# The low halves of the first expert table's 128 chunks, subtracted on GpSimd in place of VectorE

## The chip, the cores and the metric

The kernel runs on one core of a Trainium2 chip. The metric is device time in microseconds (us). The engines are called by the profile's names: PE (TensorE matmuls), PEld (TensorE weight loads), DVE (VectorE), ACT (ScalarE), POOL (GpSimd) and SP (the engine that issues most DMAs).

## The reference, cut to what matters

One layer of a latent-token backbone: two token mixers (retention and RG-LRU) over 512 latent and 256 context tokens, then a PEER feed-forward net with 16384 one-neuron experts, of which each token uses 16 in each of 8 heads. The change lies in that last part:

```
s1, i1 = lax.top_k(s[:, :, 0], K);  s2, i2 = lax.top_k(s[:, :, 1], K)
cand = (s1[..., :, None] + s2[..., None, :]).reshape(PEER_BLOCK, PEER_HEADS, K * K)
top, ci = lax.top_k(cand, K)
e = i1[ci // K] * PEER_NKEYS + i2[ci % K]          # shortened
g = jax.nn.softmax(top, axis=-1)
act = jax.nn.gelu(jnp.einsum('thkd,td->thk', u_tab[e], xb))
return jnp.einsum('thk,thkd->td', g * act, v_tab[e])
```

`u_tab` is the first table and `v_tab` the second; each has 16384 rows of 1024 floats.

## The kernel before, in words

Matmuls run in a 32-bit format of reduced precision (fp32r). To keep precision every operand x is split in two: `split` (L60) has ACT copy x rounded into a high half (L61) and DVE subtract that from x for the low half (L62). `mm3` (L64) then makes three products, high by high (L65), high by low (L66) and low by high (L67).

After the mixers (until about 640 us) the expert part has three stages.

- **Key scores and top 16** (about 680 to 820 us). PE makes the queries and the scores; DVE finds the 16 best of each half and of the pairs (`top16`, L644, and `top_pairs`, L657).
- **One-hot blocks** (822 to 1050 us). For three of the four tiles of 128 tokens the routing weights are spread into a dense table `wd`. Each tile is one block of eight groups of 16 tokens: DVE builds four one-hot tensors for a group (L887 to L890, 128x2048 fp16), PE multiplies them in 32 small products (L896, L897, into `pw`), and ACT copies these out (L898). Between the second and third block stands the preparation of the fourth token tile (`gather_prep`, L779).
- **Output** (1055 to 1850 us). For 128 chunks of 128 experts each, PE adds act times v into three output tiles (`po`, 18 products of 512 columns for a chunk). DVE makes `af` (L969) and the low halves `al` and `vwl` of it (L62). The fourth token tile is worked on beside that: POOL gathers single rows of the tables by indirect DMA into four `row` buffers (L801, L809) and DVE uses them (L803, L814).

The first table is not gathered for the three tiles but worked through densely: `s_stage` (L750) loads chunk j (512 KB, tile `w`, two buffers), splits it into `wh` and `wl` (four buffers each), makes 24 products of 384 columns into `pS` (two PSUM buffers) and has ACT apply the gelu (`gt`, L756). These 128 chunks, called S chunks here, are spread over all three stages. In the first two they fill PE between other work; in the output stage there is one for about two output chunks.

Code order doesn't set the order on the engines: a scheduler orders every engine's instructions when the kernel is built, by its own model of their cost, and each engine then works through its list in order. Buffers come free when the last reader is done. So SP's next load of a `w` tile waits for both readers of the old one, ACT's copy and the subtraction; SP works in order too.

Of the kernel before, what the change touches and what calls it, by code (L numbers as in the profile page):

```python
# [17 lines left out]
OP = mybir.AluOpType  # L18
# [34 lines left out]
def block_kernel(ctx: ExitStack, tc: tile.TileContext, A):  # L53
    nc = tc.nc
    V, S, PE, G, SY = nc.vector, nc.scalar, nc.tensor, nc.gpsimd, nc.sync

    def f(ap):
        return ap.bitcast(F32)

    def split(hi, lo, src):  # L60
        S.activation(hi, src, AF.Copy)  # L61
        V.tensor_tensor(lo, src, f(hi), op=OP.subtract)  # L62

    def mm3(out, wh, wl, xh, xl, start, stop):  # L64
        PE.matmul(out, wh, xh, start=start, stop=False)  # L65
        PE.matmul(out, wh, xl, start=False, stop=False)  # L66
        PE.matmul(out, wl, xh, start=False, stop=stop)  # L67
# [5 lines left out]
    wst = ctx.enter_context(tc.tile_pool(name="wst", bufs=2, reuse_waits="tile"))  # L73
    wsp = ctx.enter_context(tc.tile_pool(name="wsp", bufs=4, reuse_waits="tile"))
# [5 lines left out]
            return psA.tile([128, 1024], F32, name=name, tag="ps2")  # L80
        return psA.tile([128, 512], F32, name=name, tag="ps1", bufs=2)

    def load_split(src, st, sp):
        n, m = src.shape[1:]
        w = st.tile([128, n, m], F32, name="w", tag="w")
        SY.dma_start(w, src)
        wh = sp.tile([128, n, m], F32R, name="wh", tag="wh")
        wl = sp.tile([128, n, m], F32R, name="wl", tag="wl")
        split(wh, wl, w)
        return wh, wl  # L90


# [13 lines left out]
    def prefetch(n):  # L106
        while plan and len(ahead) < n:
            ahead.append(load_split(plan.pop(0), wst, wsp))
# [43 lines left out]
    st = sstk.enter_context(tc.tile_pool(name="start", bufs=1, reuse_waits="tile"))  # L152
# [95 lines left out]
    sp = const.tile([128, 24], F32, name="sp")  # L248
# [52 lines left out]
    def lru_in(c, pu, pp):  # L301
        u = lp.tile([128, NT], F32, name="u")
        S.activation(u, pu[:, :NT], AF.Identity, scale=col("conv_w", 16 + c), bias=col("conv_b", c))
        for tap, sh in ((0, 2), (1, 1), (3, -1)):
            for lo, hi in ((0, NX), (NX, NT)):
                if sh > 0:
                    o, i = u[:, lo + sh:hi], pu[:, lo:hi - sh]
                else:
                    o, i = u[:, lo:hi + sh], pu[:, lo - sh:hi]
                V.scalar_tensor_tensor(o, i, col("conv_w", 8 * tap + c), o, op0=OP.mult, op1=OP.add)  # L310
        uh = lp.tile([128, NT], F32R, name="uh")
        ul = lp.tile([128, NT], F32R, name="ul")
        split(uh, ul, u)
        x5 = lp.tile([128, NX], F32, name="x5", tag="q")
        S.activation(x5, pp, AF.Copy)
        g5 = lp.tile([128, NX], F32, name="g5")
        S.activation(g5, x5, AF.Square)
        V.tensor_scalar(g5, g5, 0.044715, 1.0, op0=OP.mult, op1=OP.add)
        V.tensor_tensor(g5, g5, x5, op=OP.mult)
        S.activation(g5, g5, AF.Tanh, scale=math.sqrt(2.0 / math.pi))  # L320
        V.scalar_tensor_tensor(g5, g5, 1.0, x5, op0=OP.add, op1=OP.mult)
        return u, uh, ul, g5
# [38 lines left out]
    def rope_split(hi, lo, p, scale=1.0):  # L361
        x = rp.tile([128, NX], F32, name="rx", tag="P", bufs=2)
        t = rp.tile([128, NX], F32, name="rt", bufs=1)
        S.activation(x, p[:, :NX], AF.Copy, scale=scale)
        for a in (0, 64):
            b = 64 - a
            V.tensor_tensor(t[a:a + 64], x[b:b + 64], ssin[b:b + 64], op=OP.mult)
        V.tensor_tensor(x, x, cos, op=OP.mult)
        V.tensor_tensor(x, x, t, op=OP.add)
        split(hi, lo, x)  # L370
# [165 lines left out]
    with ExitStack() as es:  # L536
# [53 lines left out]
        for q, (pool, th, tl) in enumerate(((lm, "lruh", "lrul"), (mg, "reth", "retl"))):  # L590
            wo.append([pool.tile([128, 4, KT, 128], F32R, name=f"wo{t}", tag=t, bufs=1) for t in (th, tl)])
            for c in range(4):
                w = wst.tile([128, KT, 128], F32, name="w", tag="w")
# [6 lines left out]
        for hf in range(2):  # L600
            if hf:
                wqs = [load_split(A["wq"][i], wst, wsp) for i in range(HG)]
            tk = slice(HN * hf, HN * hf + HN)
            ps = ps_of("ps_ss2", psW)
            for c in range(KT):
                pm = ps_of("pout", psS)
                wh, wl = (t[:, c % 4] for t in wo[c // 4])
# [141 lines left out]

    def s_stage(j):  # L750
        ps = psS.tile([128, 512], F32, name="pS")
        uh, ul = load_split(A["uT"][j], wst, wsp)
        for k in range(KT):
            mm3(ps[:, :DT], uh[:, k], ul[:, k], h2h[:, k, :DT], h2l[:, k, :DT], k == 0, k == KT - 1)
        gt = pb.tile([128, DT], F32, name="gt", bufs=RING)
        S.activation(gt, ps[:, :DT], AF.Gelu_apprx_tanh)  # L756
        if j < SPILL:
            SY.dma_start(gd[:, j], gt)
        else:
            Gs[j] = gt  # L760
# [3 lines left out]
    def s_more(n=1):  # L764
        nonlocal s_next
        for _ in range(n):
            if s_next < 128:
                s_stage(s_next)
                s_next += 1
# [284 lines left out]
```

## Time and profile before

| | us |
|---|---|
| median of 3 runs | 1881.03 (1879.26 to 1882.01) |
| profiled execution | 1879.51 |
| its span | 1877.7 |

The profile has the share of each engine in the span, the stretches in which it is busy, for every group of instructions its number, its mean time and what ended the idle time before it, and the waits of one engine on another. A matmul's time in a row is its length in a pipeline and overlaps the next one's; what one costs is the distance between starts. A mean granted TensorE clock of 1.00 is full speed.

### The profile page before, as it was taken

How to read it: one execution, taken by the hardware profiler on the slowest of the kernel's cores; microseconds unless marked ns; L12 is line 12 of the kernel's file. 1: busy time of each engine (PE TensorE's matmuls, PEld its weight loads, DVE VectorE, ACT ScalarE, POOL GpSimd, SP SyncE). 2: the span in 40 equal slices, each digit the busy share in tenths (PEclk: the TensorE clock that was granted, in tenths of full speed). 3: DMA queues.
4: the chain of work that ended last, by engine and by line, in shares of the span. 5: the costliest groups of instructions: out<-in, count | busy, mean ns of one | idle time of the engine just before them, and what ended most of it. 6: DMA issues, size and time to landing. Idle time of an engine off the chain costs nothing.

```text
span 1877.7 us, 26999 instructions
## 1 busy us (share of the span) xinstructions
PE 1820.2 (97%) x9969; PEld 1603.0 (85%) x9969; DVE 1512.3 (81%) x2801; ACT 824.3 (44%) x1213; POOL 375.7 (20%) x327
## 2 busy tenths in 40 slices
PE   7899999999999999999999999999999999999997
PEld 3788888887888989999999988888887888888885
DVE  8987878788844579999988578886786879788688
ACT  4667575765222444445545333333333333333333
POOL 0000000000000000000022134443443535445350
PEclk9999999999999999999999999999999999999999
DMA  7122121225943433567778999998989999999986
GB/s 310 52 67 68 57 68 57 68 64 189 335 136 115 138 108 115 184 193 238 261 283 299 317 345 328 345 336 298 323 324 312 346 340 337 347 331 355 319 302 208
DMA packets 175753, 432.72 MB, mean 230 GB/s; under 512 B 14082, under 2 KB 87170, under 8 KB 171140
## 3 DMA queue, kind: packets, MB, share of 16 engines
q1 hardware_dynamic: 138756, 296.75, 46.7%
q0 software_dynamic: 36864, 134.23, 19.7%
q8 instruction: 78, 1.28, 0.3%
q14 instruction: 55, 0.45, 0.1%
HBM read 389.32 MB, written 41.62 MB: 229 GB/s over the span
## 4 chain that ended last, share of the span: by engine, by line
PE 74%; DVE 11%; DMA 9%; ACT 3%; issue 2%; SPq 1%; DVEq 0%; ACTq 0%
PE po L65 8%; PE po L66 8%; PE po L67 8%; PE pS L65 7%; PE pS L66 7%; PE pS L67 7%; DMA wt<-wd 4%; DMA vw<-in_v_dram 2%; DVE wl L62 2%; PE pgm L65 1%; PE pgm L66 1%; PE pgm L67 1%; PE pmm L66 1%; PE pmm L67 1%; PE pmm L65 1%
## 5 line engine op out<-in xcount | busy, mean ns | idle before, releaser
L61 ACT ACTIVATE wh<-w 128x1024 fp32r<-128x1024 f32 (+1 forms) x216 | 224.8, 1043 | 369.0 <-DMA w<-in_uT_dram 105.0
L65 PE MATMUL pS<-h2h,wh 128*128 128x384 f32 x1024 | 347.1, 339 | 7.0 <-ACT gt L756 6.7
L67 PE MATMUL pS<-h2h,wl 128*128 128x384 f32 x1024 | 346.1, 338 | 0.7 <-DVE wl L62 0.7
L66 PE MATMUL pS<-h2l,wh 128*128 128x384 f32 x1024 | 346.2, 338 | 0.0
L62 DVE TENSOR_TENSOR wl<-w,wh 128x1024 fp32r<-128x1024 f32 (+1 forms) x216 | 259.0, 1200 | 88.2 <-ACT wh L61 87.5
L801 POOL DMA_INDIRECT row<-in_u_dram,ei x128 | 181.9, 1421 | 609.7 <-DVE row L803 316.0
L66 PE MATMUL po<-vwl,ah 128*128 128x512 f32 x768 | 299.9, 391 | 1.2 <-DVE vwl L62 1.2
L67 PE MATMUL po<-vwh,al 128*128 128x512 f32 x768 | 298.9, 390 | 0.0
L65 PE MATMUL po<-vwh,ah 128*128 128x512 f32 x768 | 271.5, 395 | 10.0 <-ACT vwh L61 8.1
L61 ACT ACTIVATE ah<-af 128x384 fp32r<-128x384 f32 x128 | 67.2, 525 | 387.0 <-PE po L66 220.2
L809 POOL DMA_INDIRECT row<-in_v_dram,ei x128 | 183.9, 1436 | 208.5 <-DVE acc L814 175.2
L65 PEld LDWEIGHTS pS<-h2h,wh 128*128 128x128 f32 x1024 | 193.2, 189 | 14.3 <-ACT gt L756 8.4
L67 PEld LDWEIGHTS pS<-h2h,wl 128*128 128x128 f32 x1024 | 193.1, 189 | 6.0 <-DVE wl L62 1.0
L66 PEld LDWEIGHTS pS<-h2l,wh 128*128 128x128 f32 x1024 | 193.3, 189 | 4.3
L62 DVE TENSOR_TENSOR vwl<-vw,vwh 128x1024 fp32r<-128x1024 f32 x128 | 156.1, 1220 | 27.1 <-ACT vwh L61 25.6
L65 PEld LDWEIGHTS po<-vwh,ah 128*128 128x128 f32 x768 | 143.1, 188 | 38.4 <-ACT vwh L61 10.6
L814 DVE SCALAR_TENSOR_TENSOR acc<-row,act,acc 128x1024 f32<-128x1024 f32 x127 | 162.7, 1281 | 14.0 <-DMA row<-in_v_dram,ei 13.4
L66 PEld LDWEIGHTS po<-vwl,ah 128*128 128x128 f32 x768 | 144.4, 188 | 29.9 <-DVE vwl L62 2.3
L67 PEld LDWEIGHTS po<-vwh,al 128*128 128x128 f32 x768 | 144.4, 188 | 27.8 <-DVE al L62 0.2
L61 ACT ACTIVATE vwh<-vw 128x1024 fp32r<-128x1024 f32 x128 | 134.4, 1051 | 61.6 <-DMA vw<-in_v_dram 59.9
L803 DVE SCALAR_TENSOR_TENSOR row<-row,h2t 128x1024 f32<-128x1024 f32 x128 | 153.8, 1220 | 2.4 <-DMA row<-in_u_dram,ei 2.4
L62 DVE TENSOR_TENSOR al<-af,ah 128x384 fp32r<-128x384 f32 x128 | 71.0, 554 | 62.6 <-ACT ah L61 57.5
(372 smaller groups left out, 3505.8 us busy)
## 6 DMA issues: line engine op xcount, KB each, us to landing
w<-in_uT_dram SPq DMA_DIRECT2D x128, 512.0 KB
vw<-in_v_dram SPq DMA_DIRECT2D x128, 512.0 KB
w<-in_w_in_dram SPq DMA_DIRECT2D x48, 512.0 KB
wd<-stg SPq DMA_DIRECT2D x24, 1024.0 KB
modb<-in_mod_t_dram SPq DMA_DIRECT2D x32, 512.0 KB
wt<-wd SPq DMA_DIRECT2D x9, 1536.0 KB
gd<-gt SPq DMA_DIRECT2D x57, 192.0 KB
gr<-gd SPq DMA_DIRECT2D x57, 192.0 KB
```

The source lines that it names most:

```text
L61: S.activation(hi, src, AF.Copy)
L62: V.tensor_tensor(lo, src, f(hi), op=OP.subtract)
L65: PE.matmul(out, wh, xh, start=start, stop=False)
L66: PE.matmul(out, wh, xl, start=False, stop=False)
L67: PE.matmul(out, wl, xh, start=False, stop=stop)
L801: G.indirect_dma_start(out=row, out_offset=None, in_=A["u"], in_offset=bass.IndirectOffsetOnAxis(ap=ei[:, j:j + 1], axis=0))
L803: V.scalar_tensor_tensor(row, row, 1.0, h2t, op0=OP.mult, op1=OP.mult, accum_out=act[:, j:j + 1])
L809: G.indirect_dma_start(out=row, out_offset=None, in_=A["v"], in_offset=bass.IndirectOffsetOnAxis(ap=ei[:, j:j + 1], axis=0))
L814: V.scalar_tensor_tensor(acc, row, act[:, j:j + 1], acc, op0=OP.mult, op1=OP.add)
```

## The change

`split` and `load_split` take an engine, and `s_stage` gives POOL for it. All other splits stay with DVE.

```
-    def split(hi, lo, src):
+    def split(hi, lo, src, eng=None):
         S.activation(hi, src, AF.Copy)
-        V.tensor_tensor(lo, src, f(hi), op=OP.subtract)
+        (eng or V).tensor_tensor(lo, src, f(hi), op=OP.subtract)
...
-    def load_split(src, st, sp):
+    def load_split(src, st, sp, eng=None):
...
-        split(wh, wl, w)
+        split(wh, wl, w, eng)
         return wh, wl
...
-        uh, ul = load_split(A["uT"][j], wst, wsp)
+        uh, ul = load_split(A["uT"][j], wst, wsp, G)
```

The scheduler lays out the instructions anew on all engines from the first S chunk on. On POOL the list after the start-up was nothing but gathers:

```order
L849 IOTA iof 128x128
L801 DMA row<-in_u_dram,ei 128x1024 x128
L809 DMA row<-in_v_dram,ei 128x1024 x128
L1050 UNCONDITIONAL_BRANCH
L1050 ISA
```

Now, in the first two stages, with `wl` the low half of an S chunk, it reads:

```order
L849 IOTA iof 128x128
L62 TENSOR_TENSOR wl<-w,wh 128x1024 x33
L801 DMA row<-in_u_dram,ei 128x1024 x4
L62 TENSOR_TENSOR wl<-w,wh 128x1024 x15
L801 DMA row<-in_u_dram,ei 128x1024 x2
L62 TENSOR_TENSOR wl<-w,wh 128x1024 x2
L801 DMA row<-in_u_dram,ei 128x1024
L62 TENSOR_TENSOR wl<-w,wh 128x1024
```

The first 33 subtractions stand ahead of the first gather, and from then on gathers and subtractions share the list; in the output stage one subtraction stands behind each three to five gathers.

On DVE, at the third group of the first one-hot block, the list was this (`ohB`, `ohAl` and `ohAh` are the one-hot tensors; `top`, `ci`, `cscr`, `prod`, `e` and `b` belong to the pair search of the next tile):

```order
L887 TENSOR_TENSOR ohB<-iota,e2T 128x2048
L888 TENSOR_TENSOR ohAl<-iota,e1T 128x2048
L647 MATCH_REPLACE cscr<-top,cand 128x50
L709 TENSOR_TENSOR prod<-mask,nlens 128x512
L890 TENSOR_TENSOR ohAl<-ohAl,glT 128x2048
L691 TENSOR_TENSOR prod<-prod 128x256
L647 MATCH_REPLACE cscr<-top,cand 128x50
L62 TENSOR_TENSOR wl<-w,wh 128x1024
L889 TENSOR_TENSOR ohAh<-ohAl,ghT 128x2048
L648 MAX top<-cscr 128x8
L691 TENSOR_TENSOR prod<-prod 128x256
L691 TENSOR_TENSOR prod<-prod 128x128
```

At that group it now reads:

```order
L887 TENSOR_TENSOR ohB<-iota,e2T 128x2048
L888 TENSOR_TENSOR ohAl<-iota,e1T 128x2048
L647 MATCH_REPLACE cscr<-top,cand 128x50
L648 MAX top<-cscr 128x8
L691 TENSOR_TENSOR prod<-prod 128x128
L693 TENSOR_TENSOR e_8001<-prod 128x64
L889 TENSOR_TENSOR ohAh<-ohAl,ghT 128x2048
L648 MAX top<-cscr 128x8
L649 MAX_INDEX ci<-top,cscr 128x8
L693 TENSOR_TENSOR b<-prod 128x64
L890 TENSOR_TENSOR ohAl<-ohAl,glT 128x2048
L649 MAX_INDEX ci<-top,cscr 128x8
```

The low half `wl` between the builds is gone, and DVE's list is otherwise of the same kinds of row. PE's list has the same products, in another order. The table says how many S chunks stand in it ahead of a place:

| S chunks ahead of | before | now |
|---|---|---|
| the first product of one-hot block 1 | 23.6 | 17.4 |
| the first product of block 2 | 39.2 | 29.4 |
| the first product of block 3 | 52.4 | 46.0 |
| the first product of the output stage | 67.9 | 66.4 |

In the output stage both lists mix the two kinds of chunk alike. There the gather that a subtraction stands right behind can start when a `row` buffer is free, which takes a DVE instruction that stands some four output chunks ahead of PE's use of that `wl`.

## Rows read from the trace of the kernel before

**Rows 1.** The page, part 1: busy us (share of the span) and count.

```profile
PE 1820.2 (97%) x9969; PEld 1603.0 (85%) x9969; DVE 1512.3 (81%) x2801; ACT 824.3 (44%) x1213; POOL 375.7 (20%) x327
```

**Rows 2.** Stretches: length, busy us (count) of each engine, clock, DMA, GB/s.

```profile
822.00:902.00 80.00, 80.00 (x624) 76.47 (x623) 79.22 (x226) 45.35 (x74) 0.00 (x0) 1.00 0.73 246
902.00:974.00 72.00, 72.00 (x591) 69.34 (x590) 65.02 (x98) 35.27 (x61) 10.51 (x4) 1.00 0.78 280
974.00:1050.00 76.00, 76.00 (x604) 73.95 (x604) 63.28 (x67) 37.28 (x62) 16.86 (x10) 1.00 0.81 284
...
1100.00:1800.00 700.00, 690.76 (x3320) 605.56 (x3319) 562.16 (x716) 244.29 (x334) 305.43 (x219) 1.00 0.94 331
```

**Rows 3.** The same stretches, DVE on tile wl alone: length, busy us (count).

```profile
822.00:902.00 80.00, 18.19 (x15) 1.00 0.73 246
902.00:974.00 72.00, 15.88 (x13) 1.00 0.78 280
974.00:1050.00 76.00, 17.75 (x15) 1.00 0.81 284
...
1100.00:1800.00 700.00, 65.90 (x54) 1.00 0.94 331
```

**Rows 4.** PE's waits, 640 us to the end: total us, times, longest.

```profile
PE po L65 <- ACT vwh L61: 8.1, 6, 2.7
PE pS L65 <- ACT gt L756: 6.7, 4, 4.1
...
PE pS L67 <- DVE wl L62: 0.7, 1, 0.7
...
PE pps L839 <- ACT sc L841: 0.2, 1, 0.2
```

**Rows 5.** PE in order of time, three places: start, length, instruction.

```profile
840.49 0.33 PE L66 MATMUL pS<-h2l,wh 128*128 128x384 f32 x1
...
841.53 0.33 PE L66 MATMUL pS<-h2l,wh 128*128 128x384 f32 x1
...
848.10 0.23 PE L897 MATMUL pw<-ohAl,ohB 128*128 128x128 f16 x1
...
848.40 0.22 PE L896 MATMUL pw<-ohAh,ohB 128*128 128x128 f16 x1
```

**Rows 6.** DVE groups: shapes, count | busy us, mean ns | idle before, releaser.

```profile
L62 DVE TENSOR_TENSOR wl<-w,wh 128x1024 fp32r<-128x1024 f32 x208 | 253.5, 1220 | 77.8 <-ACT wh L61 77.2 <-PE pw L897 0.3
...
L890 DVE TENSOR_TENSOR ohAl<-ohAl,glT 128x2048 f16<-128x2048 f16 x8 | 9.7, 1220 | 0.0
...
L812 DVE TENSOR_SCALAR acc<-row,act 128x1024 f32<-128x1024 f32 x1 | 0.8, 755 | 0.0
```

**Rows 7.** POOL groups, whole span.

```profile
L801 POOL DMA_INDIRECT row<-in_u_dram,ei x128 | 181.9, 1421 | 609.7 <-DVE row L803 316.0 <-PE pw L897 280.7 <-issue 11.8
L378 POOL IOTA dist<- 128x320 f32 x8 | 3.2, 400 | 17.8 <-DVE dt L388 9.2 <-ACT sc L396 5.7 <-ACT dt L395 2.9
L378 POOL IOTA dist<- 128x512 f32 x4 | 2.2, 560 | 11.7 <-ACT sx L383 11.7
```

**Rows 8.** S chunks finished, 736 to 800 us; what ACT's wh waited for.

```profile
L756 ACT ACTIVATE gt<-pS x13: 470/473/491, 739.8 to 798.5; 128x384 f32<-128x384 f32 x13
...
  DMA w<-in_uT_dram: 25.7, 10
```

**Rows 9.** POOL in order of time, two gathers: start, length [idle before <-releaser].

```profile
976.77 1.68 POOL L801 DMA_INDIRECT row<-in_u_dram,ei  x1 [30.70 <-DVE row L803]
...
1065.34 1.02 POOL L801 DMA_INDIRECT row<-in_u_dram,ei  x1 [25.66 <-DVE row L803]
```

**Rows 10.** DVE groups, 1100 to 1800 us: idle before, and its releasers.

```profile
L62 DVE TENSOR_TENSOR vwl<-vw,vwh 128x1024 fp32r<-128x1024 f32 x111 | 135.4, 1220 | 25.0 <-ACT vwh L61 23.5 <-issue 1.3
...
L969 DVE TENSOR_TENSOR af<-gt,wt 128x384 f32<-128x384 f32 x61 | 33.9, 555 | 27.1 <-DMA wt<-wd 26.0
```

## The prediction

> **What bounds the kernel now.** I read the shares first, then the stretches, then PE's waits. PE is busy for 97% of the span [rows 1], and in the three one-hot blocks and the output stage for all or nearly all of it: 80.00 of 80, 72.00 of 72, 76.00 of 76, 690.76 of 700 us [rows 2]. DVE is nearly as full in the first one-hot block (79.22 of 80 us) but not later (562.16 of 700 us). From 640 us on, PE's waits are eleven rows, from 8.1 us down to 0.2, some 23 us in all [rows 4]. The largest two end on ACT, behind transfers and table loads; the low half of an S chunk has one row, 0.7 us. So PE's own work sets the time, DVE is its close second in one place, and a lighter DVE can return little: that is the first thing to see.
>
> Is PE at its pace while it is busy? Six S products take 841.53 - 840.49 = 1.04 us, 0.173 us each, so a chunk of 24 needs 4.16 us. Five one-hot products take 0.30 us, 0.06 each, so a group's 32 need 1.9 us and a block's eight groups 15.2 us [rows 5]. Block 1 held 15.6 chunks before: 15.6 x 4.16 + 15.2 = 80.1 us, against 80 measured. PE runs there at its pace. In the top-16 stage it does not: twelve chunk intervals took 798.5 - 739.8 = 58.7 us, 4.89 each [rows 8], 0.73 us over the pace and 8.8 us in all.
>
> **The change, part by part.** Removed: 128 subtractions of 1.22 us on DVE [rows 6], 156 us of DVE work. As PE waits for them by 0.7 us in all [rows 4], almost nothing of that lies on the path.
>
> Added: 128 subtractions on POOL. The trace has no POOL instruction that reads a tensor. The nearest rows are the two index fills, 400 ns for 320 elements and 560 for 512 [rows 7]: 0.83 ns for an element written, and about 0.13 us fixed. One stream of 1024 is then 1.0 us, the lower end; two reads and a write one after the other are 2.7 us, the upper end. Two reads one after the other, with the write beside them, would be 1.8. I take 2.3, between the last two, since it moves three streams where the fills move one. (The Trainium skill, "GPSIMD Engine Reference", section 3.1, has 4497 ns for 2048 elements of such an instruction; half of it is an estimate of 2.25 us, with which the sum would be the same. No run here shows it yet.) On POOL's own time this fits: in the output stage it is busy for 305.43 of 700 us, and 54 subtractions add 124 us. An S chunk takes PE 4.16 us at the fastest, so 2.3 us keeps up.
>
> The unknown is whether DVE is held up while POOL reads. In the trace they never read side by side. DVE with two tensor operands takes 1220 ns for 1024 elements, with one 755 ns [rows 6]: the second operand's read is what limits it, so a further reader of the same partitions is likelier to take turns with it than to be free. The lower bound is no hold at all, the upper one is the whole POOL instruction for each chunk. I take turns on DVE's two-operand work only. In block 1 the 32 builds of four kinds, 9.7 us each [rows 6], are 38.8 of DVE's 61 us without `wl`, 64%, and much of the small work has two operands as well; I take 80%.
>
> Block 1 now: DVE's other work is 79.22 - 18.19 = 61.0 us [rows 2, 3]. PE has 12.0 chunks there in place of 15.6: 12.0 x 4.16 + 15.2 = 65.1 us. Without holds DVE still fits. With them it needs 61.0 + 12.0 x 2.3 x 0.8 = 83.1 us, **18.0 us more than PE**, and PE waits for one-hot tensors. PE's order is fixed, so it can't take later chunks in the meantime. The ends are 0, and at 2.7 us and 100% 61.0 + 32.4 - 65.1 = 28.3.
>
> Block 2: DVE 65.02 - 15.88 = 49.1 us; PE 16.6 chunks, 84.3 us. With holds 49.1 + 30.5 = 79.6 us, covered; at the upper end 93.9, so 0 to 9.6. Block 3 (to the first output product): DVE 63.28 - 17.75 = 45.5; PE 20.4 chunks, 100 us; with holds 83, covered, at the upper end 100.6, so 0 to 0.6. DVE's slack is that cover; if the holds were longer still, each further us would reach PE.
>
> Output stage: DVE 562.16 - 65.90 = 496.3 us, and 54 x 2.3 = 124 make 620 of 700. Some of its idle time ends on transfers, the 25.0 and 27.1 us of [rows 10], and can't be used; that gives 672, so it fits, with little room. Chance meetings of the two engines will pass through the two buffers of each operand now and then: I take 5 us, from 0 to 10.
>
> Top-16 stage: DVE's instructions there mostly have one tensor operand, so holds are taken as nothing. What it gives: a `w` buffer is now freed by POOL, which has nothing else to do, and not after DVE's queue, and ACT had waited 25.7 us for these loads [rows 8]. I take 4 of the 8.8 us lost to the pace, from 0 to 9. The other waits that end on DVE could give some 3 us more at best.
>
> Sum: 18.0 + 0 + 0 + 5 - 4 = +19 us on the profiled run's 1879.51 us, which is its span of 1877.7 and 1.8 around it. The median of the runs is 1.5 us longer, 1881.03, so **1900 us**. The ends: no hold and all gains, -12, 1869; the upper price and full holds, 28.3 + 9.6 + 0.6 + 10 = +48.5, 1929.
>
> A rule of the skill bears on this. In "SBUF — State Buffer", section "Who interferes with whom", a DVE instruction with two SBUF inputs and a POOL instruction that reads SBUF share a read path, and the second to start waits until the first is done. By that rule the holds are whole, and the sum is the one above rather than the lower end. No trace of before shows it: the gathers, POOL's only work beside a busy DVE, leave DVE's 1220 ns as they are.
>
> **The rivals.** *POOL's list holds the chunks up* (slower still). POOL waits at a gather until DVE has freed a `row` buffer, 30.70 and 25.66 us at two places [rows 9], and subtractions stand behind such gathers now, with SP's next `w` load behind these. Four `wl` buffers are a lead of four chunks, about 4 x 5 = 20 us with one-hot products between. Beyond that PE stops: 10.7 + 5.7 = 16 us on top, 1916 us. For it: waits over 20 us decide, and they are there. Against it: the scheduler placed gathers by the time at which it expects them to start, and in the output stage the lead is four output chunks.
>
> *No hold* (faster). DVE and POOL read without meeting. Then block 1 fits (61.0 against 65.1), the output stage has 134 us more DVE room, and the top-16 gain stays, with 4 us of other waits: -8, 1873 us. For it: nothing in the trace shows a meeting. Against it: the 755 against 1220 ns. It decides for faster as soon as a POOL subtraction costs DVE less than (65.1 - 61.0) / 12 = 0.34 us.
>
> *No difference.* The subtractions leave DVE as the change says, but the path is PE's work, which is the same to the last product; a short hold, about 0.6 us for each chunk of block 1 (3 us of waiting), cancels the gain: 1881 us.
>
> **How the numbers follow.** Holds as taken: 0.50, 1900 us. POOL's list: 0.15, 1916. No hold: 0.22, 1873. No difference: 0.13, 1881. A difference under 0.2%, 3.8 us, is about what a measurement of this kernel can't tell from none. That gives slower 0.65, same 0.13, faster 0.22. The range reaches from 1868, the lower end with all gains, to 1929, the upper price with full holds; a POOL list that jams and longer holds together lie outside, as does a DVE relief larger than PE's waits.
>
> **What would show it.** In the trace after: POOL's `wl` group near 2.3 us, longer beside one-hot builds; DVE's one-hot rows longer than 1220 ns, or gaps between them that end on nothing else; PE rows `pw` waiting for `ohB`, `ohAh` or `ohAl`, some 18 us, mostly in block 1; chunk intervals in the top-16 stage near 4.2 to 4.5 us. One-hot rows still at 1220 ns without gaps would mean no hold. PE waiting on `wl` from POOL by over 10 us, behind gathers that wait for L803, would be the second case. The forecast is wrong if the output stage takes more than some 10 us extra, since its cover was counted as holding.

## The result, and the profile after

The changed kernel takes **1968.2 us** (median of 4 runs, 1961.9 to 1972.9) beside 1881.5 us before (4 runs, 1879.3 to 1883.0): a ratio of 1.046, with a 95% interval of 1.044 to 1.049. Slower was forecast, but by 19 us; it is 87, and outside the range. The profiled execution has a span of 1960.1 us, 82.4 us more than before.

The page's first part, busy us and share of the span, answers [rows 1]:

```profile
PE 1838.0 (94%) x9969; PEld 1614.3 (82%) x9969; DVE 1567.6 (80%) x2673; ACT 824.2 (42%) x1213; POOL 704.9 (36%) x455
```

DVE lost 128 instructions, 156 us of work, and is busy for 55 us *longer* than before. So what is left on it must have grown by some 210 us. The groups of POOL and DVE (shapes and count | busy us, mean ns | idle before, with its releasers), which answer [rows 6, 7], show where:

```profile
L62 POOL TENSOR_TENSOR wl<-w,wh 128x1024 fp32r<-128x1024 f32 x128 | 329.2, 2574 | 287.5 <-ACT wh L61 285.0 <-PE pps L839 1.7
...
L803 DVE SCALAR_TENSOR_TENSOR row<-row,h2t 128x1024 f32<-128x1024 f32 x128 | 187.6, 1492 | 19.0 <-DMA row<-in_u_dram,ei 19.0
L814 DVE SCALAR_TENSOR_TENSOR acc<-row,act,acc 128x1024 f32<-128x1024 f32 x127 | 187.3, 1475 | 20.4 <-DMA row<-in_v_dram,ei 19.6
L62 DVE TENSOR_TENSOR al<-af,ah 128x384 fp32r<-128x384 f32 x128 | 91.5, 715 | 29.8 <-ACT ah L61 29.8
L889 DVE TENSOR_TENSOR ohAh<-ohAl,ghT 128x2048 f16<-128x2048 f16 x24 | 46.9, 1963 | 0.1
L890 DVE TENSOR_TENSOR ohAl<-ohAl,glT 128x2048 f16<-128x2048 f16 x24 | 39.5, 1657 | 0.2
L646 DVE FIND_INDEX8 idx<-vals,sc 128x8 uint32<-128x128 f32 x64 | 17.7, 284 | 0.0
L648 DVE MAX8 vals<-tscr 128x8 f32<-128x128 f32 x64 | 15.9, 277 | 0.0
```

The same view of the kernel before, two of these groups:

```profile
L803 DVE SCALAR_TENSOR_TENSOR row<-row,h2t 128x1024 f32<-128x1024 f32 x128 | 153.8, 1220 | 2.4 <-DMA row<-in_u_dram,ei 2.4
...
L646 DVE FIND_INDEX8 idx<-vals,sc 128x8 uint32<-128x128 f32 x64 | 17.4, 280 | 0.0
```

A build of a one-hot tensor had 1220 ns [rows 6] and has 1657 to 1963. The dot products of the gathered rows (L803) had 1220 as well and have 1492. The searches with one tensor operand (L646, L648) keep their 277 to 284 ns. Among these groups only work with two tensor operands has grown, and it has grown in busy time, not in the idle time before it: the instruction is counted as running while it is held.

Two stretches in order of time (start, length, instruction, idle before it) show how. First DVE, then POOL, in the first one-hot block:

```profile
849.96 1.21 DVE L888 TENSOR_TENSOR ohAl<-iota,e1T 128x2048 f16<-128x2048 f16 x1
851.09 0.68 DVE L717 TENSOR_TENSOR prod<-mask,dif 128x1024 f16<-128x1024 f16 x1
851.70 0.46 DVE L684 CAST cf<-ci 128x128 f16<-128x128 uint32 x1
851.83 0.76 DVE L645 MAX8 top<-cand 128x8 f32<-128x50 f32 x6
...
852.93 2.42 DVE L889 TENSOR_TENSOR ohAh<-ohAl,ghT 128x2048 f16<-128x2048 f16 x1
...
855.60 2.36 DVE L681 COPY dif<-lst 128x16 f16<-128x16 f16 x1
```

```profile
850.44 3.82 POOL L62 TENSOR_TENSOR wl<-w,wh 128x1024 fp32r<-128x1024 f32 x1 [4.44 <-ACT wh L61]
855.27 2.65 POOL L62 TENSOR_TENSOR wl<-w,wh 128x1024 fp32r<-128x1024 f32 x1 [1.02 <-ACT wh L61]
```

The first POOL subtraction ends at 850.44 + 3.82 = 854.26. Undisturbed ones have 2.36 us, so it did its work from 851.90 on: it had waited for DVE's L888 and L717, the later of which ends at 851.77. DVE's one-operand MAX8 ran beside it. L889 came at 852.93, was held until about 854.26, and then did its own work of 1.1 to 1.2 us: it ends at 855.35. The second subtraction ends at 857.92, and a DVE copy of 16 elements for each partition, 0.16 us at its fastest, stands for 2.36 us beside it. Each engine waits until the other's instruction is done, whole.

PE's waits from 640 us on (us in total, times, longest), against [rows 4]:

```profile
PE po L65 <- ACT vwh L61: 27.3, 14, 5.3
PE pS L65 <- ACT gt L756: 14.8, 7, 5.1
PE pw L897 <- DVE ohAl L890: 13.0, 9, 4.2
PE pw L896 <- DVE ohAh L889: 12.3, 6, 5.7
PE pt L865 <- DVE e L693: 8.1, 1, 8.1
...
PE pS L67 <- POOL wl L62: 1.0, 1, 1.0
```

PE waits for POOL itself by 1.0 us. What it waits for is DVE, at one-hot tensors and the pair search's `e`, and ACT, behind the loads of the second table. Of the 14.8 us on `gt`, 9.5 lie in the top-16 stage, where ACT, which works in order, stood behind loads of `w` and behind DVE's `g`; the runs don't say what share of these the holds have.

### The profile page after: what moved, and what is told of

It is laid out like the page before. It is cut to its first block, busy times and chain, and to the rows that moved or that the text cites. A ratio compares the mean times of both kernels' runs of the same rounds, so it can differ in the third digit from the quotient of the medians.

```text
span 1960.1 us, 27022 instructions
## 1 busy us (share of the span) xinstructions
PE 1838.0 (94%) x9969; PEld 1614.3 (82%) x9969; DVE 1567.6 (80%) x2673; ACT 824.2 (42%) x1213; POOL 704.9 (36%) x455
## 4 chain that ended last, share of the span: by engine, by line
PE 50%; DVE 24%; DMA 13%; issue 6%; ACT 3%; SPq 2%; POOL 2%; DVEq 0%; ACTq 0%; POOLq 0%
DMA vw<-in_v_dram 6%; PE po L66 5%; PE po L65 5%; PE po L67 5%; PE pS L67 3%; PE pS L65 3%; PE pS L66 3%; DMA row<-in_v_dram,ei 2%; SPq L957 2%; DMA wt<-wd 2%; DVE al L62 1%; PE pgm L65 1%; DVE ohAh L889 1%; PE pgm L66 1%; PE pgm L67 1%
## 5 line engine op out<-in xcount | busy, mean ns | idle before, releaser
L62 POOL TENSOR_TENSOR wl<-w,wh 128x1024 fp32r<-128x1024 f32 x128 | 329.2, 2574 | 287.5 <-ACT wh L61 285.0
L65 PE MATMUL pS<-h2h,wh 128*128 128x384 f32 x1024 | 352.2, 344 | 15.0 <-ACT gt L756 14.8
L67 PE MATMUL pS<-h2h,wl 128*128 128x384 f32 x1024 | 350.4, 342 | 1.0 <-POOL wl L62 1.0
L65 PE MATMUL po<-vwh,ah 128*128 128x512 f32 x768 | 276.9, 398 | 29.3 <-ACT vwh L61 27.3
L801 POOL DMA_INDIRECT row<-in_u_dram,ei x128 | 190.0, 1484 | 128.3 <-DVE row L803 97.6
L809 POOL DMA_INDIRECT row<-in_v_dram,ei x128 | 175.9, 1374 | 156.1 <-DVE acc L814 129.1
L814 DVE SCALAR_TENSOR_TENSOR acc<-row,act,acc 128x1024 f32<-128x1024 f32 x127 | 187.3, 1475 | 20.4 <-DMA row<-in_v_dram,ei 19.6
L803 DVE SCALAR_TENSOR_TENSOR row<-row,h2t 128x1024 f32<-128x1024 f32 x128 | 187.6, 1492 | 19.0 <-DMA row<-in_u_dram,ei 19.0
L62 DVE TENSOR_TENSOR vwl<-vw,vwh 128x1024 fp32r<-128x1024 f32 x128 | 162.8, 1273 | 40.0 <-ACT vwh L61 39.8
L62 DVE TENSOR_TENSOR wl<-w,wh 128x1024 fp32r<-128x1024 f32 (+1 forms) x88 | 104.5, 1188 | 51.8 <-ACT wh L61 48.4
```

Of the source, the lines that this page charges most:

```text
L62: (eng or V).tensor_tensor(lo, src, f(hi), op=OP.subtract)
L801: G.indirect_dma_start(out=row, out_offset=None, in_=A["u"], in_offset=bass.IndirectOffsetOnAxis(ap=ei[:, j:j + 1], axis=0))
L803: V.scalar_tensor_tensor(row, row, 1.0, h2t, op0=OP.mult, op1=OP.mult, accum_out=act[:, j:j + 1])
L809: G.indirect_dma_start(out=row, out_offset=None, in_=A["v"], in_offset=bass.IndirectOffsetOnAxis(ap=ei[:, j:j + 1], axis=0))
L814: V.scalar_tensor_tensor(acc, row, act[:, j:j + 1], acc, op0=OP.mult, op1=OP.add)
```

## The experiments

Three theories were set against each other; the last four runs set up two of their own, A and B, which their texts explain. T1: POOL's reads hold DVE. T2: POOL's own list, or `w` and `wl` buffers freed late by it, holds PE. T3: the order that the scheduler made with the new costs, or the missing DVE work, sets the time. Ratios are against the kernel before, from runs on the same chip, with the 95% interval in brackets.

**Without the subtraction, and with POOL writing only.** First, in `s_stage`:

```diff
-        uh, ul = load_split(A["uT"][j], wst, wsp, G)
+        w = wst.tile([128, KT, 128], F32, name="w", tag="w")
+        SY.dma_start(w, A["uT"][j])
+        uh = wsp.tile([128, KT, 128], F32R, name="wh", tag="wh")
+        S.activation(uh, w, AF.Copy)
+        ul = uh
```

> Leaves the low half of the S chunks out altogether: nobody subtracts, the third product takes the high half twice. DVE gets its full relief, POOL gets nothing. Theory T1 (POOL's subtraction and DVE's two-operand work take turns, and that is the loss): 1865 to 1882 us, at or a little under the kernel before. Theory T2 (the loss comes from POOL's list, in which subtractions stand behind gathers, and from SP's loads behind these): the same. Theory T3 (the scheduler's new order, with fewer S chunks ahead of the one-hot blocks, loses by itself on the chip): over 1900 us, with PE waiting for one-hot tensors and for the pair search as in the changed kernel.

1878.5 us, ratio 0.9998 [0.9982, 1.0015]. Next, in place of `ul = uh`:

```diff
+        ul = wsp.tile([128, KT, 128], F32R, name="wl", tag="wl")
+        for _ in range(3):
+            G.memset(f(ul), 0.0)
```

> Leaves the low half out: in place of the subtraction POOL fills the same low-half tile with zeros three times, about 2.6 us of POOL time that writes the tile and reads none. POOL's list, its length and the wait of PE on it stay. T1: within 15 us of the run without a low half, 1865 to 1890 us, DVE's one-hot builds back at 1.22 us. T2: most of the loss stays, over 1930 us. T3: over 1900 us.

1876.6 us, 0.9989 [0.9962, 1.0015]. POOL's and DVE's groups of this kernel:

```profile
L758 POOL MEMSET wl<- 128x1024 f32 x384 | 369.3, 965 | 224.2 <-PE pS L67 155.2 <-PE ppq L67 57.7
...
L896 DVE TENSOR_TENSOR ohAl<-ohAl,glT 128x2048 f16<-128x2048 f16 x24 | 29.3, 1229 | 0.3
```

POOL is busy with S chunks for 369 us, more than the 329 of the changed kernel, and PE's order is the new one (to within half an S chunk at each of the four places). Nothing is lost: T3 falls, and so does the part of T2 that rests on POOL's list. DVE's one-hot rows stay at 1229 ns: POOL *writing* doesn't hold two-operand work. These two runs also bound the gain: taking 156 us off DVE returns nothing there that can be told from none.

**One read instead of two.** POOL copies `w` into `wl`:

```diff
+        G.tensor_copy(ul, w)
```

> Leaves the low half out: POOL copies w into the low-half tile, one operand read in place of two, waiting for the load as before. T1 with holds as long as the POOL instruction: the copy takes 1.0 to 1.4 us against 2.57 in the changed kernel, holds shrink to about a half, 1890 to 1925 us. T1 with holds only from two-operand POOL reads: 1865 to 1885. T2: over 1930, since the list is the same. T3: over 1900.

1902.2 us, 1.011 [1.0074, 1.0145]. One row of POOL and one of DVE:

```profile
L757 POOL CAST wl<-w 128x1024 fp32r<-128x1024 f32 x128 | 173.5, 1357 | 338.4 <-PE pS L67 163.2 <-PE ppq L67 62.3 <-issue 57.8
...
L895 DVE TENSOR_TENSOR ohAl<-ohAl,glT 128x2048 f16<-128x2048 f16 x24 | 34.0, 1426 | 0.2
```

DVE's four one-hot rows have 1286 to 1426 ns. One read for each element holds DVE too, for a shorter time.

**POOL also frees `w`.** As the fills, and POOL then reads eight columns of `w`, so that the buffer waits for POOL's list:

```diff
+        G.tensor_copy(ul[:, 0, :8], w[:, 0, :8])
```

> Leaves the low half out: POOL fills the low-half tile three times and then copies 8 columns of w into it, so that POOL's list, its length and the release of w by POOL for SP's next load are as in the changed kernel, while POOL reads next to nothing. T1: as the run with the fills alone, 1865 to 1890 us. T2 (SP's loads stand behind POOL's list): over 1900.

1871.6 us, 0.9953 [0.9935, 0.997]. The rest of T2 falls: in the output stage SP waits for POOL by 134.8 us here and by 141.6 in the changed kernel. This kernel is the best mate for the changed one: PE reaches the same places in the same order (17, 29, 46 and 66 whole S chunks stand ahead of block 1, 2, 3 and the output in both; at block 2 the mate is half a chunk, about 2 us, further on), and only POOL's long reads are gone. Between those places, first the changed kernel, then this one (length, then busy us (count) of PE, PEld, DVE, ACT and POOL, clock, DMA share, GB/s; top-16 stage, blocks 1 to 3, output stage):

```profile
676.00:819.00 143.00, 122.96 (x723) 119.11 (x722) 141.34 (x753) 53.37 (x97) 49.96 (x21) 0.93 0.39 122
819.00:910.00 91.00, 71.15 (x548) 65.77 (x545) 90.86 (x215) 39.95 (x66) 35.59 (x13) 0.96 0.58 201
910.00:1008.00 98.00, 91.85 (x687) 89.49 (x688) 69.15 (x74) 41.20 (x69) 46.11 (x22) 0.97 0.64 220
1008.00:1114.00 106.00, 102.61 (x751) 99.53 (x750) 64.06 (x48) 44.66 (x73) 65.93 (x29) 1.00 0.83 273
1114.00:1960.00 846.00, 800.38 (x3782) 695.75 (x3780) 692.16 (x777) 285.69 (x399) 497.48 (x302) 0.98 0.90 311
```

```profile
676.00:794.00 118.00, 115.09 (x719) 112.02 (x719) 116.26 (x742) 52.27 (x96) 63.35 (x81) 1.00 0.47 149
794.00:862.00 68.00, 68.00 (x558) 65.91 (x558) 67.84 (x232) 39.77 (x66) 47.77 (x49) 1.00 0.72 259
862.00:952.00 90.00, 87.02 (x679) 84.77 (x678) 48.70 (x65) 40.89 (x69) 58.95 (x69) 1.00 0.72 248
952.00:1054.00 102.00, 101.37 (x749) 99.25 (x749) 40.05 (x46) 45.02 (x73) 78.95 (x91) 1.00 0.83 281
1054.00:1869.00 815.00, 790.61 (x3785) 691.02 (x3783) 588.89 (x777) 283.15 (x399) 509.46 (x480) 0.99 0.92 323
```

Row by row, the stage is longer by **25, 23, 8, 4 and 31 us**, 91 together, the whole difference of the two spans (1960.1 - 1868.9). DVE is busy for 25, 23, 20, 24 and 103 us longer, 196 together before rounding, over nearly the same instructions. Where DVE had no free time without the holds (116.26 of 118 us, 67.84 of 68), all of a hold reaches the end. Where it had (48.70 of 90, 40.05 of 102), 8 of 20 and 4 of 24 us do. In the output stage 31 of 103 do, although DVE had 226 us free.

**The subtraction on POOL in one part of the program alone**: chunks 0 to 23 (top-16 stage and the start of block 1), 24 to 66 (the rest of the blocks), 67 to 127 (output stage).

```diff
-        uh, ul = load_split(A["uT"][j], wst, wsp, G)
+        uh, ul = load_split(A["uT"][j], wst, wsp, G if j < 24 else None)
```

The other two differ in this condition alone.

> POOL subtracts for the first 24 chunks only, which lie in the top-16 stage and the first one-hot block; DVE does the other 104. T1 (turns) by the trace of the changed kernel: the stage up to the first one-hot product lost some 18 us there and the first block some 25, of which part belongs to later chunks, so +18 to +35 us. If holds cost only beside one-hot builds: 0 to +8.

> POOL subtracts for chunks 24 to 66 only, which lie in the one-hot blocks. T1: +20 to +40 us. If the loss sits in the serial pair search ahead of the first block: under +10.

> POOL subtracts for the last 61 chunks only, in the output stage. T1 with the loss that the changed kernel's trace has there: +20 to +35 us. If the output stage lost only what the late blocks handed on to it (table wd written late, loads bunched): 0 to +8.

1904.8, 1926.6 and 1908.6 us: 1.0134 [1.0117, 1.0151], 1.0249 [1.0232, 1.0266] and 1.0145 [1.0126, 1.0164]. No part is free, and their losses add up to 5.3% against 4.6% for all. The middle part lost 45 us, more than the 20 to 40 expected and than the 35 of the three block rows above; why isn't shown. In the first, PE waits for `e` of the pair search by 8.1 us, as in the changed kernel, and two of the four one-hot rows stay at 1216 and 1223 ns; in the last all four do (1216 to 1218), and L803 and L814 have the long rows: the holds go where POOL's reads are.

**Half the columns.** POOL subtracts four of a chunk's eight column blocks, DVE the others:

```diff
+        h = KT // 2
+        G.tensor_tensor(ul[:, :h], w[:, :h], f(uh[:, :h]), op=OP.subtract)
+        V.tensor_tensor(ul[:, h:], w[:, h:], f(uh[:, h:]), op=OP.subtract)
```

> GpSimd subtracts the first four of a chunk's eight column blocks, VectorE the other four; 128 GpSimd instructions as in the changed kernel, each of half the length (about 1.2 us). Theory A, a VectorE instruction waits for the rest of the GpSimd instruction that it meets, so the loss goes with GpSimd's time or faster: +1.2 to +2.6%, 1904 to 1930 us, the rows of one-hot builds between before's and after's. Theory B, a meeting costs a price of its own whatever the length: +4 to +5%, 1957 to 1975 us.

1925.8 us, 1.0225 [1.0188, 1.0261]: as many POOL instructions, half the loss, although DVE is relieved of only half the work. It goes with the length of POOL's instruction, not with how many there are.

**The hold with no relief.** The kernel before, in which POOL subtracts once more into a tile that nobody reads:

```diff
+        V.tensor_tensor(ul, w, f(uh), op=OP.subtract)
+        G.tensor_tensor(pb.tile([128, KT, 128], F32, name="w2", bufs=1), w, f(uh), op=OP.subtract)
```

> The kernel before, in which VectorE subtracts all low halves, and GpSimd subtracts each S chunk once more into a tile that nobody reads. Holds alone, with no relief: Theory A, +4.6% and more, since VectorE keeps its 156 us and its own subtraction meets GpSimd's as well: 1968 to 2040 us, VectorE's one-hot rows at 1600 ns or over. Theory B, the loss of the changed kernel comes from PE waiting on GpSimd or from the order in which the work stands now: here PE waits for VectorE's wl as before, and the time stays at 1875 to 1900 us.

2044.3 us, 1.0872 [1.0828, 1.0916], a little over the upper end expected; the one-hot rows, 1394 to 1581 ns, are shorter than expected. POOL's result is used by nobody here, so PE can't wait for it. Two groups of this kernel, and the least, middle and longest time of POOL's:

```profile
L758 POOL TENSOR_TENSOR w<-w,wh 128x1024 f32<-128x1024 f32 x128 | 373.6, 2919 | 309.0 <-ACT wh L755 266.8 <-issue 39.4 <-POOL w L758 0.7
...
L757 DVE TENSOR_TENSOR wl<-w,wh 128x1024 fp32r<-128x1024 f32 x128 | 193.3, 1512 | 30.3 <-ACT wh L755 30.3
```

```profile
L758 POOL TENSOR_TENSOR w<-w,wh x128: 2337/2559/18260, 678.8 to 1937.7; 128x1024 f32<-128x1024 f32 x128
```

DVE's own subtraction of the same chunk, released by the same `wh`, now meets POOL's: 1512 ns, and POOL's 2919. DVE is busy for 1744.8 us, 232 more than in the kernel before, over the same instructions, and the loss is nearly twice that of the change. That fits a change that takes DVE work off the path and pays more than that for it; but how much of the difference is the missing relief isn't shown, since the holds are longer too, and not only DVE's. The longest POOL subtraction, 18.26 us from 994 us on, stands behind DVE work, all but one instruction of it with two operands, that runs without a gap from 994.5 to 1010.1 us. It reads a `w` buffer all that time: SP waits 12.7 us for it with the next load, and ACT 11.1 us for that load. So T2 has a part in this run. In the changed kernel the longest POOL subtraction has 4.14 us.

**How the output stage lets the holds through.** There PE waits for `vwh`, 27.3 us, which waits for the load of `vw`, which SP can issue only when held DVE has done `vwl` and frees one of two buffers. A third buffer was put in (for the tile `xt`, which shares them, as well), once with POOL subtracting chunks 67 on, once in the kernel before:

```diff
-        v = ph.tile([128, D], F32, name="vw", bufs=2)
+        v = ph.tile([128, D], F32, name="vw", bufs=3)
```

> As e6 (GpSimd subtracts only the chunks from 67 on), with three instead of two buffers for the loads of the second table (vw). Theory A, the output stage loses because held VectorE frees vw late, so that its next load lands late and PE waits for vwh: the PE row po <- ACT vwh falls from 22.8 us to under 8, and most of e6's 27 us goes: 1878 to 1892 us. Theory B, PE loses in the stage for another reason (its order, the acc and gt chain): the wait may fall, the time stays at 1902 to 1912 us.

> The control of e8: the kernel before, VectorE subtracting everything, with three vw buffers. Its waits on vwh are 6.8 us, so both theories expect 1872 to 1882 us. If it gains as much as e8 does against e6, the third buffer is worth that by itself and e8 says nothing of the holds.

1885.8 us, 1.0011 [0.9989, 1.0033], and 1865.9 us, 0.9921 [0.9891, 0.9951], the second under the 1872 to 1882 that both theories expected. Without the control the first would have read as a proof: all but 3 of the 27 us are gone. But the buffer is worth 17 us in the kernel before by itself. Between the two kernels with three buffers some 17 to 20 us remain (0.9% by the ratios, against 1.45% with two). So only a small part of the loss, some 8 us and hardly more than the intervals, passes through these buffers. (Theory A's other sign was not quite there either: PE's wait on `vwh` is 10.1 us, not under 8.) PE's waits, from 640 us on, with POOL subtracting and three buffers:

```profile
PE po L66 <- DVE vwl L62: 14.0, 8, 5.5
PE po L65 <- ACT vwh L61: 10.1, 4, 4.0
PE po L65 <- ACT ah L61: 3.5, 1, 3.5
```

and in the control:

```profile
PE po L65 <- ACT vwh L61: 5.8, 2, 4.0
...
PE po L65 <- ACT ah L61: 0.9, 1, 0.9
```

With the load out of the way, PE waits for DVE's `vwl` itself. The three rows are 27.6 us against 6.7, 21 us more. (The two profiled executions are 30.6 us apart, the slowest of the one kernel and the fastest of the other; the medians are 20 apart.) The control is the fastest of all kernels here that compute the whole, 17 us under the kernel before, and owes nothing to POOL.

## Why the prediction was right or wrong

- *POOL's price.* Taken as 2.3 us; 2.36 alone, 2.57 in the mean, since POOL waits for DVE as well. The lower end, one stream in 1.0 us, is the fill's 0.965. Right.
- *DVE is held, on work with two tensor operands.* Right in kind. In size too: 2.3 us on 80%, 1.84 for each chunk, was taken; DVE grew by 196 / 128 = 1.53, and by 23 / 12 = 1.9 in block 1.
- *The relief is worth little.* Right: 0 to -10 us in the three kernels without long reads by POOL. The rival *No hold*, 1873 us, is what the kernel with fills and the short read gave, 1871.6.
- *Block 1, +18.* 23 against its mate. PE does wait for `ohAh` and `ohAl`, 25.3 us over the three blocks, of which 13.2 lie in block 1. The term was short because DVE's other work there was taken from the old order, 61.0 us; in the new order it is 67.8 (the mate's row).
- *Blocks 2 and 3, 0.* 8 and 4. Within the bounds for block 2, over them for block 3. The sums over a block said "covered", and most was; PE, in a fixed order, waits at the place where a hold falls, even with free time later in the block.
- *Top-16 stage, -4.* **This step failed.** It said that DVE's instructions there "mostly have one tensor operand, so holds are taken as nothing". Most by count, yes; but a hold costs what POOL's instruction lasts, not what DVE's does. The pair search's small two-operand steps, 0.2 us each, can stand for over 2 us when they meet a subtraction. Group by group against the mate, some 19 of DVE's 25 us lie in these steps and 6 in the first one-hot builds. The changed kernel's `e` and `b` rows (ns: least, middle, longest):

```profile
L693 DVE TENSOR_TENSOR e<-prod x5: 199/211/2127, 766.3 to 807.7; 128x64 f32<-128x64 f16 x5
L693 DVE TENSOR_TENSOR b<-prod x3: 161/179/2090, 766.7 to 810.0; 128x64 f16<-128x64 f16 x3
```

  And DVE had no free time there, which the prediction never looked up: 142.96 of 146 us before the change (the row below, in the form of the rows above). PE's pitch of 4.89 us for a chunk was read as a matter of loads, and DVE's share of this stage was not among [rows 2]. The stage lost 25 us, where a gain of 4 was summed.

```profile
681.00:827.00 146.00, 141.28 (x870) 137.75 (x869) 142.96 (x765) 61.47 (x108) 0.00 (x0) 1.00 0.47 149
```

- *Output stage, +5, "it fits, with little room".* **This step failed as well**, as the prediction's last sentence allowed. DVE's added time was foreseen, 124 us for 54 chunks in 700 us, and 103 came in the whole stage. The cover did not hold: nearly a third of it passed, 31 us. That two buffers of each operand between loads, ACT, DVE and PE are too short a lead for such holds is a reading that no run here shows. That the late load alone does it has fallen with the third buffer; with it, PE ends up waiting on DVE's `vwl`. How the loss divides between the chains is open.
- *PE's clock*, which the sum left out. After PE's long wait for `e` its granted clock fell. In the changed kernel (columns as above; the stretch behind PE's 8.1 us wait for `e`):

```profile
796.00:800.00 4.00, 2.80 (x17) 2.48 (x15) 4.00 (x3) 1.29 (x2) 2.25 (x2) 1.00 0.62 193
800.00:804.00 4.00, 0.00 (x0) 0.00 (x0) 4.00 (x8) 0.14 (x1) 2.50 (x1) 0.96 0.49 173
804.00:808.00 4.00, 1.13 (x5) 1.13 (x5) 4.00 (x26) 0.49 (x2) 0.00 (x0) 0.50 0.30 117
808.00:812.00 4.00, 4.00 (x18) 4.00 (x18) 4.00 (x30) 0.00 (x0) 0.00 (x0) 0.69 0.02 6
812.00:816.00 4.00, 4.00 (x25) 4.00 (x24) 4.00 (x18) 1.44 (x2) 1.82 (x1) 1.00 0.13 49
```

  In the row behind the wait PE's granted clock is 0.50, the lower of its two levels, 1.2 GHz, and from 812 on it is back at 2.4. Over the whole run the mean granted clock is 0.981, and 0.994 in the mate. The same products take PE 1838.0 us, and 1811.9 in the mate: 26 of the 91 us, about what the two clocks make of them. The other 65 are idle time.
- *POOL's list*, the rival at 1916 us: fell, with 1.0 us of waiting and with both fills. *No difference*: fell.

The direction came out because the hold was read from 755 against 1220 ns. The size did not, because 196 us of holds were set against cover that was summed over whole stages, and in one stage never looked up. Of the 72 us between the 19 of the sum and the 91 against the mate, 29 lie in the top-16 stage, 26 in the output stage, 12 in blocks 2 and 3 and 5 in block 1.

## What to carry to other kernels

Before work with two operands goes to POOL, list what DVE does with two operands (or as a fast copy) in each stage, and DVE's busy share there. Here, where that share was near 100%, every microsecond by which DVE was held was lost; where it was 40 to 70%, still a sixth to two fifths. A small instruction can be held as long as a large one. And give each buffer experiment its control: a third buffer gained some 24 us beside the holds and 17 without them.

## What the runs showed of the hardware

DVE and POOL hold each other for whole instructions, in both directions: POOL's 3.82 us above holds 1.5 us of waiting for DVE. The turns need not be even: the 18.26 us above are one POOL subtraction behind some twenty DVE instructions in a row. A POOL copy of the same tile (1.36 us in the mean) holds DVE less than a subtraction does. A POOL fill (0.965 us) holds no two-operand work, but it does hold DVE's copies and casts, of which there are few. In the kernel before (ns: least, middle, longest):

```profile
L681 DVE COPY dif<-lst x4: 141/162/169, 741.0 to 919.7; 128x16 f16<-128x16 f16 x4
L679 DVE CAST lst<-idx x4: 733/742/758, 739.1 to 883.1; 128x256 f16<-128x256 uint32 x4
```

and with POOL filling:

```profile
L681 DVE COPY dif<-lst x4: 165/530/1042, 730.0 to 853.0; 128x16 f16<-128x16 f16 x4
L679 DVE CAST lst<-idx x4: 756/992/1297, 727.8 to 825.0; 128x256 f16<-128x256 uint32 x4
```

In the kernel without the low half and without fills these have 172 and 778 in the middle. So what POOL must leave alone depends on what it does: its reads hold DVE's two-operand work, its writes hold copies and casts, and MAX8 and FIND_INDEX8 run beside both. A subtraction, which reads and writes, held at least one copy (2.36 us above). The Trainium skill has this rule in "SBUF — State Buffer", section "Who interferes with whom": DVE's second pair of ports is POOL's as well; the first to issue keeps it for its whole instruction; a two-input DVE instruction meets only POOL's reads, and copies and casts can take both ports. These runs agree on who holds whom, with the numbers above; which ports carry it no run here shows.

One thing stays unexplained: of three kernels without POOL's long reads, the one with the short extra copy was the fastest, 0.5% under the kernel before where the others were level with it.
